# GpSimd for some sums and operand differences, 48 ones columns for the row sums, and three changes of order

## The chip, the core and the metric

The kernel runs on one core of a Trainium2 chip. The metric is the time of the whole kernel on the device in microseconds (us). Three runs of the kernel before took 2451.98, 2453.47 and 2453.75 us; their median, 2453.47, is the time before. A profiled execution gives a trace: start, length and the reason for waiting of each instruction on TensorE (PE, with its weight loads as PEld), VectorE (DVE), ScalarE (ACT), GpSimd (POOL) and SyncE (SP, which only issues transfers here).

## What is computed

One step of a hybrid decoder layer on 1024 prompt tokens and 64 sample tokens (T = 1088 rows of 1024 values), in float32:

```python
def ffn_half(x, nw, wg, wu, wd):
    h = rmsnorm(x, nw)
    return x + 0.5 * ((jax.nn.silu(h @ wg) * (h @ wu)) @ wd)
# x = ffn_half(x, first weights)
# u = rmsnorm(x) @ w_in;  x = x + concat(NSA(u_att), Mamba2(u_ssm)) @ w_out
# x = ffn_half(x, second weights);  y = rmsnorm(x)
```

`rmsnorm` divides each row by the root of its mean square (over 1024 values) and multiplies by a weight. NSA is an attention with three branches, Mamba2 a scan over chunks; neither is changed. The feed-forwards have an inner width of 2816 and are the bulk of the work.

## The kernel before, in words

**Products.** Every float32 operand is split into two parts that TensorE takes at full rate: `hi` (a rounded copy, by ScalarE or VectorE, line L267) and `lo` (the rest, a subtraction, L270). A product is then three matmuls, hi by hi, hi by lo and lo by hi (`mm3`, L250 to L252). The feed-forwards' products go by the Strassen-Winograd scheme: seven half-size products in place of eight, whose operands are sums and differences of the quarters of x and of the weights.

**Layout.** x lies with its features on the partitions (eight blocks of 128) and the tokens in the free dimension. The tokens come in two halves of 544; each half is worked on in two ranges, `z = 0` (256 tokens) and `z = 1` (288). A feed-forward's right operands are the tiles `B1` to `B7`, hi and lo (`B1h`, `B1l`), each for four pairs of row blocks `kk`. For one `kk`, `b_quad` splits the four quarters into B1 to B4, and `b_rest` makes four differences in place (rows `h<-h,h`, or `xT<-xT` and `T<-xT` before the second feed-forward) and splits three of them into B5, B6, B7. `First` is the first gate or up product of a feed-forward, which runs on B1 to B4 alone (eight plain products, L412 to L414), so it can start before the differences are there.

**Gate and up, then down.** `gate_up` runs 11 pairs of products p. Its outputs are tiles `Cc`; VectorE and ScalarE take them from PSUM (L375 to L386), ScalarE applies silu (L471), VectorE multiplies by half of the gate (L474). `g_factors` makes from each result the seven operands of the down projection, splits them, and stores hi and lo to a DRAM tensor `GD` (L442, L443). `Down` loads them back (`db`, L562) with the weights (`dw`, L552), makes weight sums `ds` and splits `da`, and runs the products `dq` (L633 to L635), which are added to x (`xT`, L642).

**w_out and the second norm.** x is updated by eight row blocks of w_out for the second token range at the end of the middle part (the loop over `j` below). For each row block there are 12 matmuls (`wout`), an evacuation (L2349), a square on ScalarE (L2351, into the tiles `hp` and `hpc`, which will hold the normalised rows later), and matmuls with a column of ones that add the squares up over the partitions (`nps`, L2353). `rms_row` makes from the sums the reciprocal roots and spreads them over the partitions with matmuls `nR` (L228); `h_half` (L2330) then makes the normalised rows. Weights for the last five row blocks are loaded (`out_raw`, L1907) and split (L2345) in the loop, three buffers deep. B1 to B7 of the first token range of the second feed-forward are made beside it, and its `First` gate `g` follows.

**Order.** The program is written in a framework that reorders the instructions of each engine by a simulated timeline of its own, under the dependences and under hints: `with tc.issue_after(x)` keeps what is inside behind instruction x. Engines run their instructions in order and wait for each other by semaphores; SP's queue is in order as well. So a change in one place moves instructions in others.

## Time and profile before

| | |
|---|---|
| runs (us) | 2451.98, 2453.47, 2453.75 |
| profiled execution (us) | 2458.56 |
| its span, first to last instruction (us) | 2456.9 |
| mean granted TensorE clock | 0.985 of full |
| GpSimd's busy time (us), instructions | 442.9, 556 |
| all transfers | 379.07 MB |

A row of the trace by time reads: start in us from the span's start, length in us, engine, line, operation, output tile <- inputs, partitions x elements, count of equal neighbours in one row; in brackets the idle time ahead of it and what ended it. A count's length goes from the first start to the last end. Equal instructions overlap a little, so two of 0.41 us take 0.74. A row of the table by stretches has the busy time and number of instructions of each engine, then the granted clock, the busy share of the DMA engines and GB/s.

### The profile page before, as it was taken

What the parts mean: (1) busy time and instruction counts of PE and PEld (TensorE: products, weight loads), DVE (VectorE), ACT (ScalarE), POOL (GpSimd) and SP (SyncE); (2) the same over time, 40 slices, a digit from 0 to 9 for tenths busy, and PEclk for the clock granted to TensorE, in tenths of its full rate; (3) what the DMA queues carried; (4) which work ended last, traced back from release to release, by engine and by line L of the source; (5) the groups of instructions that cost most, each with busy time, mean ns of one, the idle gap of its engine ahead of it and who ended that gap; (6) DMA issues with size and microseconds to landing.
All of it is one profiled execution on the core that took longest, in us unless ns stands there. A gap on an engine that the chain in (4) does not pass through costs nothing.

```text
span 2456.9 us, 48129 instructions
## 1 busy us (share of the span) xinstructions
PE 2394.8 (97%) x18866; PEld 2224.7 (91%) x18866; DVE 1748.7 (71%) x3833; ACT 1134.3 (46%) x2501; POOL 442.9 (18%) x556
## 2 busy tenths in 40 slices
PE   7999999999999999999999999999999999999998
PEld 6999999999999999998777775777999999999998
DVE  6767676768767855565767676778876777768776
ACT  7545444441124245333766767445544444443113
POOL 0000000011125343352545444011000000001110
PEclk9899999999999999999999999999899999999999
DMA  4434343488662333333212114476234443469654
GB/s 158 140 121 173 122 171 121 156 320 315 238 214 75 137 107 109 118 91 128 69 35 70 35 45 162 132 254 225 64 136 150 136 159 128 168 233 363 235 206 153
DMA packets 233903, 379.07 MB, mean 154 GB/s; under 512 B 18893, under 2 KB 148089, under 8 KB 233292
## 3 DMA queue, kind: packets, MB, share of 16 engines
q1 hardware_dynamic: 210248, 318.02, 38.0%
q0 software_dynamic: 11056, 38.59, 4.9%
q10 hardware_dynamic: 12372, 19.38, 2.2%
q8 instruction: 149, 2.44, 0.4%
q14 instruction: 78, 0.64, 0.1%
HBM read 255.66 MB, written 124.40 MB: 155 GB/s over the span
## 4 chain that ended last, share of the span: by engine, by line
PE 87%; DVE 5%; DMA 3%; ACT 3%; issue 1%; POOL 0%; SPq 0%; ACTq 0%; DVEq 0%; POOLq 0%
PE gY L367 6%; PE gY L366 6%; PE gY L368 6%; PE dq L633 6%; PE dq L634 6%; PE dq L635 6%; PE gX L367 5%; PE gX L366 5%; PE gX L368 5%; PE o L1862 3%; PE pT L1853 3%; PE g L414 1%; PE xbc L250 1%; PE g L412 1%; PE xbc L251 1%; PE xbc L252 1%
## 5 line engine op out<-in xcount | busy, mean ns | idle before, releaser
L633 PE MATMUL dq<-db,da 128*128 128x256 f32 (+1 forms) x1232 | 350.0, 288 | 5.0 <-DMA db<-GD 2.3
L634 PE MATMUL dq<-db,da 128*128 128x256 f32 (+1 forms) x1232 | 353.3, 288 | 0.0
L635 PE MATMUL dq<-db,da 128*128 128x256 f32 (+1 forms) x1232 | 353.0, 288 | 0.0
L270 POOL TENSOR_TENSOR ds<-dw 128x512 f32<-128x512 f32 x22 | 29.1, 1321 | 1231.8 <-DMA dw<-in_ffn_wd_dram 509.0
L642 DVE TENSOR_TENSOR xT<-xT,dq 128x256 f32<-128x256 f32 (+1 forms) x456 | 187.4, 433 | 87.1 <-PE dq L635 85.5
L633 PEld LDWEIGHTS dq<-db,da 128*128 128x128 f32 x1232 | 230.6, 189 | 6.1 <-ACT da L267 2.7
L635 PEld LDWEIGHTS dq<-db,da 128*128 128x128 f32 x1232 | 232.9, 189 | 0.0
L634 PEld LDWEIGHTS dq<-db,da 128*128 128x128 f32 x1232 | 231.9, 188 | 0.1
L267 ACT CAST whi<-ws 128x512 fp32r<-128x512 f32 x156 | 96.5, 623 | 206.0 <-PE gY L368 137.9
L270 DVE TENSOR_TENSOR wlo<-raw,whi 128x512 fp32r<-128x512 f32 x184 | 125.6, 687 | 82.8 <-ACT whi L267 82.5
L267 ACT CAST da<-ds 128x512 fp32r<-128x512 f32 x88 | 52.6, 623 | 236.0 <-PE dq L635 94.0
L267 ACT CAST whi<-raw 128x512 fp32r<-128x512 f32 x181 | 112.4, 625 | 71.9 <-PE wout L252 20.3
L270 DVE TENSOR_TENSOR wlo<-ws,whi 128x512 fp32r<-128x512 f32 x156 | 106.7, 687 | 42.4 <-ACT whi L267 39.8
L1826 DVE CUSTOM_DVE_ANT_0 pb<-s,mrow 128x384 f32<-128x384 f32 (+3 forms) x160 | 78.2, 513 | 32.5 <-PE pT L1853 15.7
L1853 PEld LDWEIGHTS pT<-ident,pb 128*128 128x128 f32 x528 | 60.3, 142 | 45.3 <-issue 37.3
L1831 ACT ACTIVATE pb<-pb,mx 128x384 f32<-128x384 f32 (+3 forms) x160 | 92.1, 577 | 17.4 <-DVE mx L1826 9.5
L366 PE MATMUL gY<-B3h,whi 128*128 128x256 f32 (+1 forms) x320 | 91.5, 286 | 1.4 <-ACT whi L267 1.4
L277 POOL TENSOR_TENSOR pb<-pb,sm 128x640 f32<-128x640 f32 (+7 forms) x70 | 84.6, 1232 | 44.2 <-DVE sm L1838 21.0
L366 PE MATMUL gX<-B6h,whi 128*128 128x256 f32 (+1 forms) x320 | 91.3, 286 | 0.7 <-ACT Cc L373 0.7
L367 PE MATMUL gX<-B6h,wlo 128*128 128x256 f32 (+1 forms) x320 | 91.4, 286 | 0.6 <-DVE wlo L270 0.6
L367 PE MATMUL gY<-B3h,wlo 128*128 128x256 f32 (+1 forms) x320 | 91.6, 287 | 0.2 <-DVE wlo L270 0.2
L367 PE MATMUL gY<-B2h,wlo 128*128 128x256 f32 (+1 forms) x320 | 91.4, 286 | 0.0
(762 smaller groups left out, 8542.1 us busy)
## 6 DMA issues: line engine op xcount, KB each, us to landing
db<-GD SPq DMA_DIRECT2D x42, 1632.0 KB
GD<-Cc SPq DMA_DIRECT2D x154, 272.0 KB
GD<-his SPq DMA_DIRECT2D x84, 272.0 KB
raw<-in_ffn_wu_dram SPq DMA_DIRECT2D x22, 1024.0 KB
dw<-in_ffn_wd_dram SPq DMA_DIRECT2D x44, 512.0 KB
raw<-in_ffn_wg_dram SPq DMA_DIRECT2D x21, 1024.0 KB
GD<-hp SPq DMA_DIRECT2D x70, 272.0 KB
db<-GD SPq DMA_DIRECT2D x14, 1088.0 KB
```

The costliest lines, as they stand in the source:

```text
L267: return nc.scalar.copy(out, src) if eng == "a" else ENGINES[eng].tensor_copy(out, src)
L270: ENGINES[eng].tensor_tensor(out, x, y, op=op)
L277: nc.gpsimd.tensor_tensor(out, x, by.to_broadcast(list(x.shape)), op=OP.mult)
L366: nc.tensor.matmul(q, ah[:, k], b_, start=first, stop=False, skip_group_check=True)
L367: nc.tensor.matmul(q, al[:, k], b_, start=False, stop=False, skip_group_check=True)
L368: nc.tensor.matmul(q, ah[:, k], c_, start=False, stop=(k == 3), skip_group_check=True)
L633: nc.tensor.matmul(q, x, bh[:, u, o], start=first, stop=False, skip_group_check=True)
L634: nc.tensor.matmul(q, y, bh[:, u, o], start=False, stop=False, skip_group_check=True)
L635: nc.tensor.matmul(q, x, bl[:, u, o], start=False, stop=(u == np_ - 1), skip_group_check=True)
L642: nc.vector.tensor_tensor(x, x, q, op=OP.subtract if i == 4 else OP.add)
L1831: nc.scalar.activation(p_, s if mask is None else p_, AF.Exp, bias=mx[:, 0:1], scale=1.0 if mask is None else -1.0, accum_out=part[:, hh_, ...
L1853: nc.tensor.transpose(tq_[:kn, P * hh_:P * hh_ + P], src, ident)
```

## The change

1. The row sums of squares (`rms_row`, `gate_sums`) are matmuls with 48 columns of ones (one column, broadcast) in place of one; the first column of each group is read.
2. In the last w_out loop the 24 matmuls `nps` (two records each in the trace) go. GpSimd adds the eight squares up in SBUF (seven additions of 128x288) and one `rms_row` on the total takes three matmuls at the end.
3. `rms_row` is cut in two, `rms_columns` (up to the reciprocal) and `rms_out` (the matmuls `nR`); for the first token range of the second norm `rms_out` is issued behind the seventh row block's products.
4. The loads of the second feed-forward's first gate and up weights (1 MB each) are issued on SP's queue behind the last two w_out loads (256 KB each), one behind each.
5. `b_rest` takes an engine: for every second row block GpSimd makes the four differences (eight of 128x256 and eight of 128x288 before the first feed-forward, eight of 128x256 before the second).
6. For the second-last p, `g_factors` makes all differences first and stores the operands in the order 6, 7, 5, 4, 1, 2, 3.

```diff
@@ -24,6 +24,7 @@
 KD = DM // P
 FB = 2816 // P
 HALF = T // 2
+NW = 48
 SUBS = [(0, 256), (256, 288)]
 CHUNKS = [(0, 384), (384, 384), (768, 320)]
 XCHUNKS = [(h * HALF + o, n) for o, n in SUBS for h in range(2)]
@@ -219,15 +220,17 @@
 
     roots = []
 
-    def norm_rows(r, parts, R):
+    def norm_columns(r):
 
         nc.vector.tensor_scalar(r, r, 1.0 / DM, EPS, op0=OP.mult, op1=OP.add)
         root = nc.scalar.activation(r, r, AF.Sqrt)
         nc.vector.reciprocal(r, r)
+        roots.append(root.ins)
+
+    def norm_rows(r, parts, R):
         for i, p0, c0, m in parts:
             nc.tensor.matmul(R[:, c0:c0 + m], r[p0:p0 + m, i:i + 1].to_broadcast([m, P]), ident[p0:p0 + m, p0:p0 + m],
                              start=True, stop=True, skip_group_check=True)
-        roots.append(root.ins)
         return R
 
     def wsplit(W, loads, early=False, dve=False):
@@ -249,7 +252,7 @@
     def mm3(q, w, xh, xl, first, last):
         nc.tensor.matmul(q, w[0], xh, start=first, stop=False)
         nc.tensor.matmul(q, w[1], xh, start=False, stop=False)
-        nc.tensor.matmul(q, w[0], xl, start=False, stop=last)
+        return nc.tensor.matmul(q, w[0], xl, start=False, stop=last)
 
     def dense(q, w, t0, n):
         for k in range(KD):
@@ -442,6 +445,15 @@
             nc.sync.dma_start(at[:, 0], f32(hi))
             nc.sync.dma_start(at[:, 1], src)
         sub("v", t1, b12, b11)
+        if p == FB // 2 - 2:
+            sub("v", t2, b22, t1)
+            yield
+            sub("v", t3, b22, b12)
+            sub("v", t4, t2, b21)
+            for x in ((6, t2), (7, t3), (5, t1), (4, t4), (1, b11), (2, b21), (3, b22)):
+                yield
+                put(*x)
+            return
         put(1, b11)
         yield
         sub("v", t2, b22, t1)
@@ -678,6 +690,7 @@
                                      accum_out=r2[p0:p0 + m, z, i:i + 1])
             parts.append((i, p0, c0, m))
         nc.vector.tensor_tensor(r, r2[:, 0], r2[:, 1], op=OP.add)
+        norm_columns(r)
         norm_rows(r, parts, R)
         Rs[t0] = FX.tile("xRs", [P, 288], 2)
         nc.scalar.copy(Rs[t0][:, :n], R[:, :n])
@@ -710,7 +723,7 @@
             due.append(x_block(s, kk))
             product(kk)
             if kk in (1, 2):
-                b_rest(s, *due.pop(0))
+                b_rest(s, *due.pop(0), "vp"[kk - 1])
         return due
 
     def late():
@@ -748,7 +761,7 @@
             u.run(0, kk, bankx, heng="v" if kk else "a")
             if kk < 2:
                 x_rms(HALF * kk + c0, n)
-                b_rest(0, *due.pop(0))
+                b_rest(0, *due.pop(0), "vp"[kk])
         with tc.issue_after(roots[-1]):
             g.finish(0)
         u.run(0, 3, bankx, heng="v")
@@ -758,7 +771,7 @@
         for kk in range(4):
             u.run(1, kk, banky)
             if kk in (0, 1):
-                b_rest(1, *due.pop(0))
+                b_rest(1, *due.pop(0), "vp"[kk])
         b_last(1)
         return [g, u]
 
@@ -840,26 +853,31 @@
         else:
             late_rows.append(m)
 
-    def rms_row(v, n, q=None, out=None):
-        out = v if out is None else out
-
+    def rms_row(v, n, out=None):
+        rms_out(*rms_columns(v, n), v if out is None else out)
+
+    def rms_columns(v, n):
         parts = blocks(n)
-        if q is None:
-            q = side("nps")
-            for i, m in parts:
-                nc.tensor.matmul(q[:m, i:i + 1], v[:, P * i:P * i + m], ones[:, :1], start=True, stop=True,
-                                 skip_group_check=True)
+        q = side("nps")
+        for i, m in parts:
+            nc.tensor.matmul(q[:m, NW * i:NW * i + NW], v[:, P * i:P * i + m], ones.to_broadcast([P, NW]), start=True,
+                             stop=True, skip_group_check=True)
+        sums = q[:, :NW * len(parts)].rearrange("p (i w) -> p i w", w=NW)[:, :, 0]
         r = NP.tile([P, len(parts)], F32, name="nr")
         if n % P:
             nc.vector.memset(r, 1.0)
-            nc.vector.tensor_copy(r[:n % P, n // P:], q[:n % P, n // P:len(parts)])
-        nc.vector.tensor_copy(r[:, :n // P], q[:, :n // P])
+            nc.vector.tensor_copy(r[:n % P, n // P:], sums[:n % P, n // P:])
+        nc.vector.tensor_copy(r[:, :n // P], sums[:, :n // P])
+        norm_columns(r)
+        return r, q, parts, n
+
+    def rms_out(r, q, parts, n, out):
         R = norm_rows(r, [(i, 0, P * i, m) for i, m in parts[:4]], side("nR"))
         nc.scalar.copy(out[:, :min(512, n)], R[:, :min(512, n)])
         for i, m in parts[4:]:
-            nc.tensor.matmul(q[:, 8:8 + m], r[:m, i:i + 1].to_broadcast([m, P]), ident[:m, :m],
+            nc.tensor.matmul(q[:, 256:256 + m], r[:m, i:i + 1].to_broadcast([m, P]), ident[:m, :m],
                              start=True, stop=True, skip_group_check=True)
-            nc.scalar.copy(out[:, 512:n], q[:, 8:8 + m])
+            nc.scalar.copy(out[:, 512:n], q[:, 256:256 + m])
 
     with pool("psum_dn", bufs=8, space=PSUM) as PD:
         adds = D1.add_x()
@@ -1347,12 +1365,13 @@
         for j, c in enumerate(cs):
             L = P if c < 8 else TS
             for g in range(2):
-                nc.tensor.matmul(q[:L, 2 * j + g:2 * j + g + 1], hs[:, j, g, :L], ones[:, :1], start=True, stop=True,
-                                 skip_group_check=True)
+                nc.tensor.matmul(q[:L, NW * (2 * j + g):NW * (2 * j + g) + NW], hs[:, j, g, :L], ones.to_broadcast([P, NW]),
+                                 start=True, stop=True, skip_group_check=True)
+        q = q[:, :6 * NW].rearrange("p (c g w) -> p c g w", g=2, w=NW)[:, :, :, 0]
         n = len(cs) - (8 in cs)
-        nc.vector.tensor_copy(yr[:, cs[0]:cs[0] + n], q[:, :2 * n].rearrange("p (c g) -> p c g", g=2))
+        nc.vector.tensor_copy(yr[:, cs[0]:cs[0] + n], q[:, :n])
         if 8 in cs:
-            nc.vector.tensor_copy(yr[:TS, 8], q[:TS, 2 * n:2 * n + 2])
+            nc.vector.tensor_copy(yr[:TS, 8], q[:TS, n])
 
     def gate_norm(yr):
         nc.vector.tensor_scalar(yr, yr, 1.0 / 256, EPS, op0=OP.mult, op1=OP.add)
@@ -1902,10 +1921,12 @@
     def two(v):
         return v.rearrange("p (b t) -> p b t", b=2)
 
+    out_loads = []
+
     def out_raw(k0, m):
         raw = WA.tile([P, 4, P], F32, name="raw", bufs=3)
-        nc.sync.dma_start(raw, A["w_out"][0][512 * k0:512 * k0 + 512, P * m:P * m + P].rearrange(
-            "(k p) f -> p k f", p=P))
+        out_loads.append(nc.sync.dma_start(raw, A["w_out"][0][512 * k0:512 * k0 + 512, P * m:P * m + P].rearrange(
+            "(k p) f -> p k f", p=P)))
         return raw
 
     def out_w(W, k0, m, eng="v", raw=None):
@@ -2234,8 +2255,8 @@
     def side(name):
         return PO.tile([P, 512], F32, name=name, tag="wout")
 
-    def x2_rms(z, q=None):
-        rms_row(acc2[z], 2 * SUBS[z][1], q)
+    def x2_rms(z):
+        rms_row(acc2[z], 2 * SUBS[z][1])
         c0, n = SUBS[z]
         for b in range(2):
             for m in range(0, KD, 4):
@@ -2330,15 +2351,17 @@
         nc.vector.scalar_tensor_tensor(rows[m][:, r], X2[1][:, m, r], wn2[:, m:m + 1], acc[:, r],
                                        op0=OP.mult, op1=OP.mult)
 
-    rms_row(a0, 288, out=acc)
+    first = rms_columns(a0, 288)
     h0 = [h_of(X2[0][:, kk], X2[0][:, kk + 4]) for kk in range(4)]
-    sums = side("nps")
     ws = kept[5:]
     raws = [out_raw(0, m) for m in MB[:3]]
     for j, m in enumerate(MB[5:] + MB[:5]):
         q = (PO if j < 6 else PL).tile([P, 512], F32, name="wout")[:, :288]
         for k in range(4):
-            mm3(q, (ws[j][0][:, k], ws[j][1][:, k]), ha[0][:, k], ha[1][:, k], k == 0, k == 3)
+            done = mm3(q, (ws[j][0][:, k], ws[j][1][:, k]), ha[0][:, k], ha[1][:, k], k == 0, k == 3)
+        if j == 6:
+            with tc.issue_after(done.ins):
+                rms_out(*first, acc)
         if j < 5:
             raw = raws[j] if j < 3 else out_raw(0, MB[j])
             hi, lo = (WA.tile([P, 4, P], F32R, name=nm_) for nm_ in ("whi", "wlo"))
@@ -2349,9 +2372,10 @@
         nc.vector.tensor_tensor(X2[1][:, m, b1_], X2[1][:, m, b1_], q, op=OP.add)
         sq = rows[m][:, b1_]
         nc.scalar.activation(sq, X2[1][:, m, b1_], AF.Square)
-        for i, n in blocks(288):
-            nc.tensor.matmul(sums[:n, i:i + 1], sq[:, P * i:P * i + n], ones[:, :1], start=(j == 0 and i == 0),
-                             stop=(j == KD - 1), skip_group_check=True)
+        if j:
+            nc.gpsimd.tensor_tensor(total, total, sq, op=OP.add)
+        else:
+            total = sq
     for i, a in ((4, 2), (3, 3), (1, 0), (2, 1)):
         for kk in range(4):
             hi, lo = (t[:, kk] for t in BN[0][i])
@@ -2365,12 +2389,12 @@
                     copy("a", hi, src)
                 with tc.issue_after(behind[1].ins):
                     sub("v", lo, src, f32(hi))
-    rms_row(acc[:, b1_], 288, sums)
+    rms_row(total, 288, out=acc[:, b1_])
     for m in range(0, KD, 4):
         nc.sync.dma_start(xD[:, m:m + 4, HALF + 256:T], X2[1][:, m:m + 4, b1_])
     with tc.issue_after(behind[1].ins):
         for kk in range(4):
-            b_rest(0, kk, h0[kk])
+            b_rest(0, kk, h0[kk], "vp"[kk % 2])
     for kk in range(4):
         for m in (kk, kk + 4):
             with tc.issue_after(behind[1].ins):
@@ -2392,7 +2416,8 @@
         return PY.tile([P, 512], F32, name=name, tag="Y", bufs=4)
 
     def begin2():
-        g = First(F1, A["ffn2_wg"][0], silu_out)
+        with tc.issue_after(out_loads[-2].ins):
+            g = First(F1, A["ffn2_wg"][0], silu_out)
         for kk in range(4):
             g.run(0, kk, bankx)
         h1 = [h_of(rows[kk], rows[kk + 4]) for kk in range(4)]
@@ -2400,7 +2425,8 @@
             b_quad(1, kk, h1[kk])
         for kk in range(2):
             b_rest(1, kk, h1[kk])
-        u = First(F1, A["ffn2_wu"][0], times_out(g))
+        with tc.issue_after(out_loads[-1].ins):
+            u = First(F1, A["ffn2_wu"][0], times_out(g))
         for kk in range(4):
             u.run(0, kk, bankx)
         for kk in range(2, 4):
```

How this moves instructions, at three places (lines of the changed program are some 3 to 23 higher: L270 is L273 there, L250 to L252 are L253 to L255, L228 is L232, L2349 is L2372, L386 is L389, L384 is L387, L474 is L486).

TensorE at the end of w_out, before: the sums stand between the sixth row block's last matmul and the seventh's first.

```order
L252 MATMUL wout<-ol,whi 128x288
L228 MATMUL nR<-ident,nr 128x128 x2
L228 MATMUL nR<-ident,nr 128x32
L2353 MATMUL nps<-ones,hp 128x1 x2
L2353 MATMUL nps<-ones,hp 32x1
L2353 MATMUL nps<-ones,hp 128x1 x2
L2353 MATMUL nps<-ones,hp 32x1
L2353 MATMUL nps<-ones,hpc 128x1 x2
L2353 MATMUL nps<-ones,hpc 32x1
```

TensorE there after, from the seventh row block's last matmuls on.

```order
L255 MATMUL wout<-ol,whi 128x288
L232 MATMUL nR<-ident,nr 128x128 x2
L232 MATMUL nR<-ident,nr 128x32
L254 MATMUL wout<-oh,wlo 128x288
L255 MATMUL wout<-ol,whi 128x288
```

The matmuls `nR` have moved behind the seventh block, and no sums are left there; three `nps` of 48 columns come 28 matmuls of the gate later.

GpSimd between the sample attention's gathers and the down projection's `ds`, after (before, nothing stands there). `hp<-hp` rows are the additions of squares, the others differences.

```order
L2376 TENSOR_TENSOR hp<-hp 128x288
L273 TENSOR_TENSOR xT_19998<-xT_19998 128x256 x3
L2376 TENSOR_TENSOR hp<-hp,hpc 128x288
L273 TENSOR_TENSOR xT_19998<-xT_19998 128x256 x2
L2376 TENSOR_TENSOR hp<-hp 128x288
L273 TENSOR_TENSOR T_21000<-xT_19998 128x256
L273 TENSOR_TENSOR xT_19998<-xT_19998 128x256
L2376 TENSOR_TENSOR hp<-hp 128x288
L273 TENSOR_TENSOR T_21000<-xT_19998 128x256
L2376 TENSOR_TENSOR hp<-hp 128x288
L2376 TENSOR_TENSOR hp<-hp,hpc 128x288 x2
```

Fifteen instructions are new on GpSimd there, in the order in which they run; the eight differences were on VectorE's queue, between the splits of the second feed-forward's operands.

VectorE at the first feed-forward's end, where the down projection's weights are prepared between the last evacuations, before:

```order
L270 TENSOR_TENSOR da_6240<-dw_6248,da_6240 128x512
L384 TENSOR_TENSOR Cc<-Cc,gY 128x288
L386 TENSOR_TENSOR Cc<-Cc,gY 128x288
L270 TENSOR_TENSOR ds_6272<-dw_6248,dw_6252 128x512
L474 SCALAR_TENSOR_TENSOR Cc<-Cc 128x1088
L386 TENSOR_TENSOR Cc<-Cc,gY 128x256
L270 TENSOR_TENSOR ds_6276<-ds_6272,dw_6248 128x512
L270 TENSOR_TENSOR Cc<-Cc 128x544
L386 TENSOR_TENSOR Cc<-Cc,gY 128x288
```

and after:

```order
L486 SCALAR_TENSOR_TENSOR Cc<-Cc 128x1088
L389 TENSOR_TENSOR Cc<-Cc,gY 128x256
L273 TENSOR_TENSOR Cc<-Cc 128x544
L273 TENSOR_TENSOR da_6240<-dw_6248,da_6240 128x512
L389 TENSOR_TENSOR Cc<-Cc,gY 128x288
L273 TENSOR_TENSOR Cc<-Cc,his 128x544
L273 TENSOR_TENSOR ds_6272<-dw_6248,dw_6252 128x512
L389 TENSOR_TENSOR Cc<-Cc,gY 128x256
L273 TENSOR_TENSOR ds_6276<-ds_6272,dw_6248 128x512
L389 TENSOR_TENSOR Cc<-Cc,gY 128x288
```

The multiplication over 1088 tokens, the difference and one evacuation that stood behind the split of the weights `dw_6248` now stand ahead of it.

## The prediction

> **What bounds the kernel now.** I read the page's busy shares and chain first, then the table by stretches at the places that the change touches, then single instructions there.
>
> ```profile
> span 2456.9 us, 48129 instructions
> PE 2394.8 (97%) x18866; PEld 2224.7 (91%) x18866; DVE 1748.7 (71%) x3833; ACT 1134.3 (46%) x2501; POOL 442.9 (18%) x556
> PE 87%; DVE 5%; DMA 3%; ACT 3%; issue 1%; POOL 0%; SPq 0%; ACTq 0%; DVEq 0%; POOLq 0%
> 20.00:40.00 20.00, 17.50 (x129) 16.31 (x128) 19.44 (x55) 15.31 (x47) 0.00 (x0) 0.91 0.50 156
> 515.00:520.00 5.00, 2.86 (x12) 2.86 (x13) 4.96 (x9) 2.65 (x6) 0.00 (x0) 0.72 1.03 356
> 1719.00:1743.00 24.00, 20.46 (x107) 19.78 (x107) 21.20 (x59) 12.14 (x35) 0.00 (x0) 0.64 0.31 104
> ```
>
> TensorE is busy 97% of 2456.9 us and stands for 87% of the chain, so only stretches where it waits, or runs at a low granted clock, can be shortened. The stretch rows (PE, PEld, DVE, ACT, POOL busy, clock, DMA share, GB/s) show three that the change touches: the first feed-forward's beginning (VectorE 19.44 of 20 us), its hand-over to the down projection (clock 0.72), and the end of w_out (clock 0.64). GpSimd does nothing in any of them. The profiled execution took 2458.56 us; the runs' median is 2453.47, so I subtract from 2453.5. The measurement tells 0.2%, or 4.9 us, from no change.
>
> **The end of w_out, where most of the change lies.**
>
> ```profile
> 1720.65 1.04 PE L228 MATMUL nR<-ident,nr 128*128 128x128 f32 x6 [1.59 <-DVE nr L226]
> 1721.63 1.98 PE L2353 MATMUL nps<-ones,hp 128*128 128x1 f32 x12
> 1724.67 3.47 PE L2353 MATMUL nps<-ones,hp 128*128 128x1 f32 x18
> 1728.07 0.85 PE L250 MATMUL wout<-oh,whi 128*128 128x288 f32 x2
> 1735.60 2.27 PE L2353 MATMUL nps<-ones,hpc 128*128 128x1 f32 x12 [1.96 <-ACT hpc L2351]
> 1737.79 0.58 PE L413 MATMUL g<-B1h,wlo 128*128 128x256 f32 x1
> 1742.44 0.33 PE L414 MATMUL g<-B3l,whi 128*128 128x256 f32 x1
> 1742.60 0.28 PE L412 MATMUL g<-B1h,whi 128*128 128x256 f32 x1
> ```
>
> The removed sums occupy TensorE from 1721.63 to 1728.07 and from 1735.60 to 1737.79: 6.4 + 2.2 us, at half clock. It looks like 8.6 us to gain. But the real work behind them waits for VectorE, whose queue has no gap here:
>
> ```profile
> 1717.03 0.74 DVE L270 TENSOR_TENSOR B2l<-xT,B2h 128x256 fp32r<-128x256 f32 x2
> 1719.41 0.74 DVE L270 TENSOR_TENSOR xT<-xT 128x256 f32<-128x256 f32 x2
> 1720.08 0.43 DVE L2349 TENSOR_TENSOR xT<-xT,wout 128x288 f32<-128x288 f32 x1
> 1725.50 0.67 DVE L2345 TENSOR_TENSOR wlo<-raw,whi 128x512 fp32r<-128x512 f32 x1
> 1734.29 2.48 DVE L270 TENSOR_TENSOR wlo<-raw,whi 128x512 fp32r<-128x512 f32 x4
> ```
>
> The first of the four splits at 1734.29, with the usual 0.69 us, ends at 1734.98; the second feed-forward's gate cannot multiply with it sooner, though the 12 sums ahead of it held it until 1737.79. So what counts is when this split ends. Two subtractions of 128x256 take 0.74 us and one 0.41, so one costs 0.335 in the queue. The change takes eight of them (blocks 1 and 3) out from ahead of the split: 8 x 0.335 = 2.7 us, and 1734.98 becomes 1732.3. The h rows and evacuations stay ahead of it, and the earlier w_out load helps the next-to-last product only if VectorE lets it.
>
> Against that stand fourteen GpSimd instructions, eight subtractions and six of the seven sums, in the same stretch; the last sum follows the last product. Their price is read elsewhere:
>
> ```profile
> 737.02 0.77 DVE L823 SCALAR_TENSOR_TENSOR hl<-xT,vec,hh 128x544 fp32r<-128x544 f32 x1
> 730.51 0.41 DVE L642 TENSOR_TENSOR xT<-xT,dq 128x256 f32<-128x256 f32 x1
> 730.90 1.42 DVE L823 SCALAR_TENSOR_TENSOR hl<-xT,vec,hh 128x544 fp32r<-128x544 f32 x1
> 729.95 1.79 POOL L270 TENSOR_TENSOR ds<-dw,ds 128x512 f32<-128x512 f32 x1
> 731.71 1.85 POOL L816 TENSOR_TENSOR rms<-rms,scr 128x544 f32<-128x544 f32 x1
> 985.62 0.74 POOL L270 TENSOR_TENSOR ea<-ea,xbc 128x256 f32<-128x256 f32 x1
> ```
>
> A VectorE operation with both inputs in SBUF takes 0.77 us alone, and 1.42 beside GpSimd: it starts at 730.90 and ends at 732.32, 0.58 after the GpSimd one (729.95 + 1.79) is done. The next GpSimd one, issued at 731.71, takes 1.85 and waits in turn for that VectorE operation. The evacuation at 730.51, with an input in PSUM, keeps its 0.41 inside GpSimd's 1.79. So the two take turns, one instruction each, and a GpSimd instruction holds VectorE for its length less the start-up that both hide in waiting, about 0.14 (0.74 becomes 0.60). The SBUF — State Buffer page of the Trainium skill, section "SBUF: two separate sides", says the same of two SBUF inputs against a GpSimd operation that reads SBUF: whichever starts first holds the shared ports for the whole instruction and the other blocks. By that rule the sum is the one that I make here, and by a split of bandwidth it would be the first rival; the rows bear the rule out.
>
> Fourteen times 0.60 is 8.4 us. About 2 us of it falls beside evacuations and waits (six evacuations like the one at 1720.08, 0.37 each in the queue), which leaves 6.4: the split ends not at 1732.3 but at 1738.7. The next-to-last product's own split is late in the same way. From the 1717.03 row the new order has one subtraction and one evacuation more (0.7), then 0.67 + 0.37 + 1.0 + 0.1 + 0.34 + 0.6 up to its end: 1720.8. Ten of the fourteen stand ahead of it, 6.0 less 0.8 of cover: 1726. So TensorE stands idle about 7 us from 1719 and comes out at half clock. The gate's first 22 matmuls then run from about 1739.0 at 0.214 us to the next edge of the clock at 1742.5 (16 of them), six more at 0.114: done at 1743.2, against 1742.55 now. Net **+0.7 us**. Ends: without any turn-taking 1732.3, 16 matmuls at half clock to the edge at 1735.7 and six at full, 1736.4: -6. With a full 0.74 and no cover, 14 x 0.74 = 10.4: the split ends at 1742.7, 22 x 0.214 more, 1747.4: +5. I stay by the middle, since the rows show both the turns and the cover.
>
> What follows there is hidden: the new sum needs the last square, GpSimd's addition (0.74 x 288/256 = 0.83) and six short matmuls; 28 gate matmuls (28 x 0.114 = 3.2 us or more) stand ahead of it on TensorE, and its norm is needed only by the second token range. If that cover went it would cost up to 2 us. On SP's queue the first w_out load now goes ahead of the two 1 MB loads, so gate's raw comes some 2 us later; it is cast at 1726.88 now and would have 10 us to spare.
>
> **48 columns.** No row has 48, but both neighbours:
>
> ```profile
> L850 PE MATMUL nps<-ones,acc x14: 165/250/250, 1623.4 to 1713.3; 128*128 128x1 f32 x12, 128*32 128x1 f32 x2
> L228 PE MATMUL nR<-ident,nr x36: 270/275/376, 763.6 to 1745.5; 128*128 128x128 f32 x32, 32*128 32x32 f32 x4
> ```
>
> One column takes 250 ns, 128 take 275, so a widened one costs 0 to 0.025 us; some 70 remain, 0 to 1.8 us. I take 0: the weight load sets the pace. The splitting of the norm reorders, and moves a few matmuls past nine others: 0 +-1.
>
> **The hand-over to the down projection.**
>
> ```profile
> 511.31 1.31 DVE L270 TENSOR_TENSOR da<-dw,da 128x512 fp32r<-128x512 f32 x1 [1.67 <-ACT da L267]
> 512.54 0.44 DVE L384 TENSOR_TENSOR Cc<-Cc,gY 128x288 f32<-128x288 f32 x1
> 513.27 0.68 DVE L270 TENSOR_TENSOR ds<-dw,dw 128x512 f32<-128x512 f32 x1
> 513.87 1.28 DVE L474 SCALAR_TENSOR_TENSOR Cc<-Cc 128x1088 f32<-128x1088 f32 x1
> 515.07 0.41 DVE L386 TENSOR_TENSOR Cc<-Cc,gY 128x256 f32<-128x256 f32 x1
> 516.64 0.44 DVE L386 TENSOR_TENSOR Cc<-Cc,gY 128x288 f32<-128x288 f32 x1
> 517.01 0.72 DVE L270 TENSOR_TENSOR Cc<-Cc,his 128x544 fp32r<-128x544 f32 x1
> 517.14 0.58 PE L633 MATMUL dq<-db,da 128*128 128x256 f32 x1 [2.26 <-DVE Cc L386]
> 513.73:517.15 3.42, 1.16 (x11) 0.93 (x9) 3.42 (x7) 2.44 (x5) 0.00 (x0) 1.00 0.74 272
> 517.15:520.56 3.41, 3.41 (x15) 3.41 (x16) 3.37 (x5) 1.54 (x4) 0.00 (x0) 0.50 1.01 312
> 540.00:545.00 5.00, 5.00 (x42) 5.00 (x41) 3.65 (x9) 1.24 (x2) 1.29 (x1) 1.00 0.74 241
> 555.00:560.00 5.00, 4.28 (x35) 4.05 (x33) 5.00 (x12) 0.62 (x2) 0.00 (x0) 1.00 1.02 402
> ```
>
> A wait for a transfer stops VectorE until 511.31, and what is queued behind it makes the last evacuation late (516.64), for which TensorE stands 2.26 us and loses the clock for the next 3.41 us (0.50, 1.7 us of work). In the new order the halving (L474, 1.28) stands ahead of the waiting instruction, and five things between 512.54 and the last evacuation: two evacuations (0.44, 0.41), a Cc remainder (0.72) and two ds (0.68), each about 0.08 less in the queue, 2.53 together. So it starts at 515.07, 1.57 earlier. TensorE's wait falls to 0.69, the stretch is busy for four fifths, and the half clock goes: -1.57 - 1.7 = -3.3. But the DMA engines are at 1.01 to 1.03 in the rows from 515 and from 555, with 0.74 between at 540 to 545, and the next wait is already theirs: within 555 to 560 TensorE is busy 4.28 of 5. A TensorE that is 3.3 us early meets transfers that are at most 1.5 early. I take **-1.5**, ends 0 and -3.3. The second feed-forward's hand-over gets the same order, at full clock: 0 to -1, **-0.3**.
>
> **The two beginnings.** Of sixteen subtractions in the first, four or five fall where VectorE is the bound (up to 37 us): each saves 0.335 there and holds VectorE 0.60 when it meets an operation with two SBUF inputs, about six in ten: 5 x (0.36 - 0.335) is nothing, ends -1.5 and +1.3. The others lie beside TensorE that is busy throughout (50 to 77 us) and are hidden; if that cover goes, eleven times 0.27 are 3 us. I take **+0.3**.
>
> The sum: 0.7 - 1.5 - 0.3 + 0.3 = -0.8, **2452.7 us**, within 0.2%.
>
> **Rivals.** First, GpSimd costs VectorE next to nothing: -6 at w_out, and with the hand-overs' -1.8 to -3.6 some 2445. The evacuation row at 730.51 speaks for it, the slow rows against it. Second, the turns cost their full length: +5 at w_out, +2 in the beginnings, -1.8 at the hand-overs: 2458.7. It decides once the blocked time exceeds some 8 us of the stretch; the chained dependences (ScalarE casts what GpSimd subtracts, in a fixed order) speak for it, the evacuations against. Third, w_out as I have it, but the transfers follow, and the hand-overs bring 3.3 + 1: 2450.2, still within the bound. Fourth, a half-clock stretch comes or goes elsewhere (each 1.7 us); it widens all cases. A page rule bears on it: TensorE: Matmul & The Clock Gate in the Trainium skill, Part 1, gives an idle window of about 3.4 us as the cause of half rate; the 3.41 us above agree.
>
> **How the numbers follow.** My case with the third: 0.53, of which the fourth carries 0.04 beyond the bound on either side. First rival 0.27, of it 0.24 beyond; second 0.20, of it 0.16 beyond. That makes faster 0.28, same 0.52 (0.45 + 0.03 + 0.04), slower 0.20. Eight in ten lie from 2445 to 2459, the ends of the first two rivals; the likeliest case alone goes from 2449 to 2456.
>
> **What would show it.** Right: VectorE's operations with two SBUF inputs at 1719 to 1738 take 0.6 to 1.0 instead of 0.41; TensorE idles 6 us or more there; the gate starts within 1.5 us of 1739 on today's scale; the half clock at 517 is gone; the wait for db near 559 has grown. Wrong: VectorE's durations there stay 0.41, or the gate starts before 1736.

## The result, and the profile after

The changed kernel takes 2465.27 us (median of 7 runs, 2459.56 to 2475.15), the kernel before 2452.96 in runs beside it (7 runs, 2447.99 to 2454.37): a ratio of 1.0051, interval 1.0036 to 1.0066. It is slower by half a per cent, outside the predicted range. The profiled execution took 2470.7 us, its span is 2469.0.

The page's first lines and the same three stretches as before:

```profile
span 2469.0 us, 48067 instructions
PE 2384.9 (97%) x18824; PEld 2215.2 (90%) x18824; DVE 1753.4 (71%) x3809; ACT 1133.2 (46%) x2501; POOL 471.4 (19%) x587
PE 83%; DMA 6%; DVE 6%; ACT 3%; issue 1%; POOL 0%; SPq 0%; ACTq 0%; DVEq 0%; POOLq 0%
20.00:40.00 20.00, 17.04 (x119) 15.94 (x119) 18.31 (x47) 14.77 (x46) 4.83 (x6) 0.83 0.46 146
515.00:520.00 5.00, 5.00 (x43) 5.00 (x41) 3.32 (x6) 3.21 (x9) 1.29 (x1) 1.00 0.99 339
1719.00:1743.00 24.00, 16.15 (x94) 14.40 (x92) 24.00 (x53) 15.95 (x40) 12.11 (x13) 0.85 0.49 159
```

TensorE is busy 9.9 us less than before in a span that is 12.1 longer, and DMA's share of the chain has doubled, from 3 to 6%. At 515 TensorE no longer stands and has its full clock (as it has in a second profile of the kernel before, told of below). At w_out's end VectorE has no gap in 24 us, beside 12.11 us of GpSimd.

To see where time goes, equal matmuls of TensorE are paired between two profiles, and the difference of their starts is followed: a **shift**, the median over slices of 25 us. Against the profile shown of before, the shift is -2.5 us behind the first beginning, -6.5 at 600, -6.95 at 1575, **+8.5 at 1700**, +11.55 at 1800 and +12.1 at the end. So most of the loss is made between 1580 and 1700, in the sample attention, a stretch that the prediction does not speak of. These are two rows of it, of the changed kernel, and then of a second profile of the kernel before (span 2455.4 us, the twelfth run below):

```profile
1620.00:1640.00 20.00, 16.04 (x164) 14.12 (x165) 13.68 (x35) 6.46 (x13) 5.12 (x5) 0.91 0.65 211
1680.00:1700.00 20.00, 14.78 (x128) 11.24 (x127) 10.42 (x36) 7.03 (x17) 2.67 (x3) 0.87 0.77 238
```

```profile
1620.00:1640.00 20.00, 20.00 (x256) 16.45 (x256) 18.07 (x47) 9.40 (x17) 7.93 (x7) 1.00 0.84 267
1680.00:1700.00 20.00, 17.79 (x184) 11.19 (x182) 11.77 (x36) 8.18 (x20) 1.38 (x2) 1.00 0.52 165
```

Nothing of the change is written there. But the framework's simulated timeline orders this stretch differently: by a count in the two traces (rows with the same operation, tiles and shape, in order), some 105 of VectorE's 558 rows between 1450 and 1716 stand elsewhere. In the list of the waits of TensorE and VectorE between 1580 and 1715 (us in total, times, longest) the changed kernel has

```profile
PE kT_ps L2092 <- DMA schk<-in_cache_win_dram: 3.9, 1, 3.9
PE sPT_ps L2150 <- DVE pcT L270: 3.1, 1, 3.1
PE so L2160 <- DVE sPT L270: 2.0, 3, 1.0
PE so L2157 <- DVE sPT L270: 1.9, 1, 1.9
DVE xs L2301 <- DMA xs<-xD: 6.7, 3, 3.7
```

and these are the places of the two long ones, by time, VectorE's ahead of TensorE's:

```profile
1697.71 0.46 DVE L2301 TENSOR_TENSOR xs<-xs,wout 128x288 f32<-128x288 f32 x1 [3.72 <-DMA xs<-xD]
1698.08 0.28 DVE L270 COPY pcT<-sPT_ps 127x128 f32<-127x128 f32 x1
1698.51 1.09 PE L2150 MATMUL sPT_ps<-ident,S 128*128 128x128 f32 x4 [3.10 <-DVE pcT L270]
1623.48 1.11 PE L2092 MATMUL kT_ps<-ident,schk 128*128 128x128 f32 x4 [3.94 <-DMA schk<-in_cache_win_dram]
```

The rows `xs` of x go from DRAM through w_out's addition back to DRAM, three buffers deep. At 1697.71 VectorE stands 3.72 us for such a load; the copy `pcT`, on which TensorE waits, is queued behind it. In the second profile of before the corresponding wait totals 2.1 us, and TensorE never waits longer than 0.5 us for VectorE there:

```profile
PE kT_ps L2071 <- DMA schk<-in_cache_sel_dram,idx: 2.7, 4, 1.8
PE so L2139 <- DVE sPT L267: 0.5, 1, 0.5
DVE xs L2280 <- DMA xs<-xD: 2.1, 1, 2.1
```

The four waits shown of the changed kernel's TensorE make 10.9 us, to which come three stretches of 3.41 us at half clock (from 1623.28, 1694.96 and 1698.37). Set against the second profile of before, waits and half clock are nearly the whole loss: between the places of 1575 and 1700 TensorE stands 12.4 us instead of 3.5, and of its 10.2 us at half clock, where that profile has none, it is busy 6.9, which is 3.5 us of work. The 8.9 and the 3.5 make 12.4 of the 13.0 us that the table below gives.

### The profile page after: what moved, and what is told of

It is laid out like the page before. It is cut to its first block, busy times and chain, and to the rows that moved or that the text cites. A ratio compares the mean times of both kernels' runs of the same rounds, so it can differ in the third digit from the quotient of the medians.

```text
span 2469.0 us, 48067 instructions
## 1 busy us (share of the span) xinstructions
PE 2384.9 (97%) x18824; PEld 2215.2 (90%) x18824; DVE 1753.4 (71%) x3809; ACT 1133.2 (46%) x2501; POOL 471.4 (19%) x587
## 4 chain that ended last, share of the span: by engine, by line
PE 83%; DMA 6%; DVE 6%; ACT 3%; issue 1%; POOL 0%; SPq 0%; ACTq 0%; DVEq 0%; POOLq 0%
PE gY L370 6%; PE gY L371 6%; PE gY L369 6%; PE dq L645 6%; PE dq L646 6%; PE dq L647 6%; PE gX L370 5%; PE gX L369 5%; PE gX L371 5%; PE o L1881 3%; PE pT L1872 3%; PE xbc L253 1%; PE xbc L254 1%; PE xbc L255 1%; DMA schk<-in_cache_sel_dram,idx 1%
## 5 line engine op out<-in xcount | busy, mean ns | idle before, releaser
L273 POOL TENSOR_TENSOR ds<-dw 128x512 f32<-128x512 f32 x22 | 29.4, 1337 | 1096.5 <-DMA dw<-in_ffn_wd_dram 880.4
L270 ACT CAST whi<-ws 128x512 fp32r<-128x512 f32 x156 | 96.4, 623 | 208.1 <-PE gY L371 137.5
L273 DVE TENSOR_TENSOR wlo<-raw,whi 128x512 fp32r<-128x512 f32 x184 | 126.4, 693 | 83.6 <-ACT whi L270 83.5
L270 ACT CAST da<-ds 128x512 fp32r<-128x512 f32 x88 | 52.3, 624 | 235.8 <-issue 96.0
L270 ACT CAST whi<-raw 128x512 fp32r<-128x512 f32 x181 | 112.3, 625 | 78.3 <-PE wout L255 22.0
L273 DVE TENSOR_TENSOR wlo<-ws,whi 128x512 fp32r<-128x512 f32 x156 | 106.7, 688 | 44.4 <-ACT whi L270 44.0
L369 PE MATMUL gY<-B2h,whi 128*128 128x256 f32 (+1 forms) x320 | 91.4, 286 | 0.0
```

Of the source, the lines that this page charges most:

```text
L270: return nc.scalar.copy(out, src) if eng == "a" else ENGINES[eng].tensor_copy(out, src)
L273: ENGINES[eng].tensor_tensor(out, x, y, op=op)
L369: nc.tensor.matmul(q, ah[:, k], b_, start=first, stop=False, skip_group_check=True)
```

## The experiments

One table for all runs. The columns are what each stretch added to the shift, in us, against the **second** profile of before, since the first has half clock from 52.94 to 76.83 which no other run with an unchanged beginning shows for so long. That second execution took 2457.09 us, some 3.5 above the median of the runs beside it, so a total that is worked out from the table looks that much better than the times do. The last two are the median time and its ratio to before with the interval.

| run | to 75 | 75 to 600 | 600 to 1575 | 1575 to 1700 | 1700 to 1800 | rest | us | ratio |
|---|---|---|---|---|---|---|---|---|
| the change | 1.4 | -2.9 | -1.5 | **13.0** | 2.5 | 1.1 | 2465.27 | 1.0051 (1.0036 to 1.0066) |
| e1 beginning + hand-over | 2.5 | -3.9 | -0.8 | **15.1** | -3.1 | 0.1 | 2464.68 | 1.0046 (1.0033 to 1.0060) |
| e2 w_out parts | 0.6 | 0.4 | -0.3 | -1.3 | **6.5** | 4.0 | 2464.78 | 1.0052 (1.0038 to 1.0066) |
| e3 hand-over | -0.2 | -3.2 | 3.3 | -2.4 | -1.6 | 0.2 | 2453.30 | 1.0001 (0.9991 to 1.0012) |
| e4 beginning | 1.9 | -1.2 | 1.8 | -0.9 | -0.1 | 0.9 | 2459.86 | 1.0035 (1.0022 to 1.0048) |
| e5 sums on VectorE | 1.5 | 0.4 | -3.0 | -0.9 | -0.4 | -0.3 | 2456.69 | 1.0011 (1.0000 to 1.0023) |
| e6 sums on TensorE | -0.2 | -0.5 | -2.6 | 0.6 | -1.4 | 1.2 | 2454.07 | 1.0004 (0.9989 to 1.0019) |
| e7 GpSimd sums only | 1.0 | -0.6 | 1.7 | -1.3 | 1.9 | 2.6 | 2457.89 | 1.0025 (1.0011 to 1.0040) |
| e8 all but 48 and hand-over | 2.0 | 0.4 | 2.7 | -1.7 | 4.4 | 0.4 | 2465.08 | 1.0047 (1.0031 to 1.0062) |
| e9 change, sums on VectorE | 0.9 | -3.6 | -1.3 | **12.6** | 0.2 | 0.4 | 2467.47 | 1.0062 (1.0045 to 1.0079) |
| e10 no GpSimd sums, no beginning | -0.5 | -2.7 | -1.9 | -0.7 | -1.2 | 0.1 | 2448.97 | 0.9985 (0.9976 to 0.9994) |
| e11 48 + hand-over | 1.1 | -3.4 | -2.0 | -0.6 | -1.0 | -0.4 | 2450.73 | 0.9998 (0.9987 to 1.0010) |
| e13 change, four xs | 2.1 | -3.8 | -3.7 | 7.9 | 4.8 | 0.3 | 2467.18 | 1.0051 (1.0032 to 1.0069) |
| e14 e10, four xs | -0.2 | -3.6 | -2.7 | 1.7 | -1.4 | 0.3 | 2450.61 | 0.9986 (0.9974 to 0.9998) |

The middle column (600 to 1575) holds code that none of the runs means to touch, and it goes from -3.7 to +3.3, with stretches of half clock that come and go. That is what one profile can be off by, so only larger differences, or ones that several runs repeat, are read as causes below.

**Is it the order in the sample attention?** First two halves of the change: the first beginning and the hand-overs (the first half of part 5, and 6), and w_out with the second beginning (2, 3, 4 and the second half of 5), each with one column of ones.

```diff
 e1: before, with
+                b_rest(s, *due.pop(0), "vp"[kk - 1])
+                b_rest(0, *due.pop(0), "vp"[kk])
+                b_rest(1, *due.pop(0), "vp"[kk])
+        if p == FB // 2 - 2:
```

> Only two parts of the change: GpSimd's differences in the first feed-forward's beginning, and the other order of the second-last p's operands. Nothing at the end of w_out, one ones column. But the scheduler now puts the sample attention (some 1600 to 1700 us) in nearly the order of the changed kernel. Theory A (the lost time comes from the order of matmuls in the sample attention): the two parts win 2.5 + 4 us by 750 us and lose 12 to 16 between 1580 and 1710: 2453 - 6.5 + 14 = about 2460. Theory B (it comes from GpSimd's work and the new sum at the end of w_out): 2453 - 6.5 = about 2446.5, no loss between 1580 and 1710.

```diff
 e2: the change, with
-NW = 48
+NW = 1
-                b_rest(s, *due.pop(0), "vp"[kk - 1])
+                b_rest(s, *due.pop(0))
-                b_rest(0, *due.pop(0), "vp"[kk])
+                b_rest(0, *due.pop(0))
-                b_rest(1, *due.pop(0), "vp"[kk])
+                b_rest(1, *due.pop(0))
-        if p == FB // 2 - 2:
+        if p < 0:
```

> Only the parts at the end of w_out: squares summed by GpSimd, the first norm's matmuls moved, w_out loads ahead of the 1 MB loads, GpSimd's eight differences before the second feed-forward. One ones column. The sample attention keeps the order of the kernel before. Theory A: no loss between 1580 and 1700, and 0.7 to 5 us (3 in the changed kernel's trace) at the end of w_out: 2454 to 2458. Theory B: 12 to 18 us slower, 2465 to 2471.

e1 has the new order in the sample attention and lost 15.1 us there, without any edit between 600 and 1700 (its time, 2464.68, is above the 2460 of its theory A, whose beginning was to win 2.5 us and lost as much). e2 has the old order, lost nothing there, but 6.5 us at the end of w_out. So there are two losses, not one. (e2's time, 2464.78, is that of its theory B, whose place is wrong. Another 4.0 us of its profile are lost behind 1800, all of it between 2150 and 2225, at the second feed-forward's hand-over, with half clock from 2189.8 to 2196.6; e7 below loses 2.2 in the same place. Why is not shown.) Then the two halves of e1, each alone; both have the old order in the sample attention.

```diff
 e3: before, with
+        if p == FB // 2 - 2:
 e4: before, with
+                b_rest(s, *due.pop(0), "vp"[kk - 1])
+                b_rest(0, *due.pop(0), "vp"[kk])
+                b_rest(1, *due.pop(0), "vp"[kk])
```

> Only the other order of the second-last p's operands. The sample attention keeps its order but for a few VectorE rows. From the changed kernel's trace the hand-over at 500 to 530 us wins 3.3 to 4 us, and the half-clock stretch at 517 us is gone: theory A says 2449 to 2450. If the hand-over's gain belonged to GpSimd's differences in the beginning instead (theory B of this step), 2453.

> Only GpSimd's sixteen differences in the first feed-forward's beginning. The sample attention keeps its order. From the changed kernel's trace: 2.5 us faster by 80 us and no change after that, 2450.5. The prediction's step said +0.3 (2453.5).

Neither loses anything between 1575 and 1700, though together they lose 15.1 there. e3 gains its 3 us at the hand-over and has given them back by 975, with half clock from 762 and from 981, where the second profile of before has none; its time is the same as before, not the 2449 to 2450 of its theory A. e4 came out 9 us above what was expected of it. Its beginning costs 1.9 us, against 0.4 in the mean of the eight runs with an unchanged beginning; the six runs with GpSimd there have 0.9 to 2.5, 1.8 in the mean, so the part costs some 1.4 us. In all its profile lies 2.5 us behind the second one of before, which with that one's 3.5 makes the 6 of its time; only the 1.4 to 1.9 are found at the beginning, the rest stays open.

Last the counter-test: nearly everything in, but a combination for which the order in the sample attention stays the old one.

```diff
 e8: the change, with
-NW = 48
+NW = 1
-        if p == FB // 2 - 2:
+        if p < 0:
```

> All of the change but the 48 columns and the new order at the hand-overs. In this one the lists of instructions in the sample attention (1580 to 1710) stand as in the kernel before, although GpSimd's differences in the first beginning are in. Theory 'the 15 to 17 us at 1580 to 1710 come from the order in those lists': they are gone, within 2 us of before there; w_out's end loses 5 to 8 us, the beginning 1 to 2: 2463 to 2467 in all. Rival 'the GpSimd work of the beginnings, or a run's chance, makes that loss, whatever the order': some 15 us lost between 1580 and 1710 again, 2475 or more.

It lost nothing between 1575 and 1700 (-1.7) with all GpSimd work in. In all sixteen profiles the stretch costs 7.9 to 15.1 us in the four with the new order (the change, e1, e9, e13) and -2.5 to 1.7 in the twelve others. By the count used above, 104 to 111 of VectorE's 558 rows moved in those four, and 0 to 9 in eleven of the others; the twelfth, e14, has a third order (97 moved) and is told of next.

**What in the new order costs it?** One more xs buffer, in the changed kernel (e13) and in e10, told of below (e14). The first pair of lines stands for three places in the program.

```diff
-        xs = WA.tile([P, 576], F32, name="xs", bufs=3)
+        xs = WA.tile([P, 576], F32, name="xs", bufs=4)
-            pg = KC.tile([P, 128], F32, name="pg")
+            pg = KC.tile([P, 128], F32, name="pg", bufs=1)
```

> The whole change with four buffers for the rows that w_out's second part loads, adds to and stores again (xs: load from DRAM, addition, store), instead of three; one small tile of the sample attention (pg) has one buffer instead of two to make room. The lists keep the changed kernel's order up to the place from which the rows are loaded ahead. Theory 'in the new order TensorE and VectorE stand behind round trips of xs through DRAM (VectorE waits 6.7 us for such loads there, in a second profile of the kernel before 2.1)': the loads start a buffer earlier, those waits go, and of 13 to 15 us between 1580 and 1710 some 5 to 8 come back; 2456 to 2461 in all. Rival 'the order of the sample attention's own chain (keys, scores, probabilities) makes the loss, xs only stands in it': under 2 us come back, 2463 to 2467.

> The kernel of the tenth run (48 columns, later norm, order of loads, second beginning's differences on GpSimd, new order at the hand-overs; no sums on GpSimd, first beginning on VectorE) with four xs buffers in the same way. That kernel waits little for xs, as the kernel before does (2.1 us of VectorE, little of it on the path): 2447 to 2449, no difference. Rival: the fourth buffer moves the order of the sample attention again, and 5 us or more are lost there.

In e13 VectorE waits for xs loads as little as in the kernel before, and the waits on `pcT` are gone:

```profile
DVE xs L2301 <- DMA xs<-xD: 2.3, 1, 2.3
PE kT_ps L2092 <- DMA schk<-in_cache_sel_dram,idx: 6.1, 5, 2.6
PE kT_ps L2092 <- DMA schk<-in_cache_win_dram: 2.5, 1, 2.5
```

The stretch costs 7.9 us instead of 13.0. That the 5 us were the round trips is likely but not shown: the fourth buffer changed the lists as well (33 of VectorE's 516 rows between 1450 and 1716 stand elsewhere than in the changed kernel). The rest is in waits for the gathered keys (`schk`, 8.6 us in all), which the new order makes longer and which this run does not explain. The time did not follow: 2467.18 us, since 2.3 us more were lost at w_out's end in its profile, and the rest is not visible in it. So these waits are seen to go in their place, and their worth in the total is not shown. In e14 the fourth buffer moved 104 of VectorE's 544 rows between 1450 and 1716 against e10, about as many as the change moves, and the time is no different from e10's (2450.61; the stretch costs 1.7 us against -0.7). So it is not reordering as such that costs 13 us, but this order; which of its moves do it stays open.

**The end of w_out.** e2 says that the w_out parts cost 6.5 us by themselves. Three runs take them apart. In e5 VectorE makes the seven sums of squares, in e6 TensorE as before, and only the eight differences are GpSimd's; in e7 only the sums are.

```diff
 e5: e2, with
-            nc.gpsimd.tensor_tensor(total, total, sq, op=OP.add)
+            nc.vector.tensor_tensor(total, total, sq, op=OP.add)
 e6: e2, with the accumulating matmuls nps of the kernel before
 e7: e2, with
-            b_rest(0, kk, h0[kk], "vp"[kk % 2])
+            b_rest(0, kk, h0[kk])
```

> The earlier run of the w_out parts (sums and differences on GpSimd, one ones column, before's order in the sample attention) lost 7.0 us between 1710 and 1775 and ended at 2464.8. Here the seven sums of squares are VectorE's, at 0.41 us each (0.335 in its queue: 2.3 us), and only the eight differences of the second feed-forward's first operands stay with GpSimd. Theory 'turns, and a dense VectorE stream keeps GpSimd out': the sum that stood 6.06 us on GpSimd while VectorE ran without a gap takes 0.41 us, six blockings of some 0.6 us are gone; the stretch 1710 to 1775 loses 2 to 4 us instead of 7, in all some 2460. Rival 'the place of the instructions does not matter, the order of the split and the casts does': 7 us lost again, some 2464 to 2466.

> As the run before, but the sums of squares stay with TensorE in the accumulating form of the kernel before; the norm's later place, the order of the loads and the eight differences on GpSimd are kept. Theory 'turns': eight blockings of 0.6 us against eight subtractions of 0.335 saved, +2.1 us, and TensorE has its sums again, which lie in time in which it waits anyway: the stretch 1710 to 1775 loses 1 to 3 us, in all 2455 to 2458. Rival 'GpSimd's differences are the whole loss, the sums nothing': 6 to 7 us lost, 2460 to 2464.

> The sums on GpSimd, but all sixteen differences of the second feed-forward's first operands on VectorE as before. Theory 'turns': six blockings of 0.6 us with nothing saved on VectorE's list, 3 to 4 us; the last sum waits on GpSimd for a gap in VectorE's stream again (3 to 6 us, of which what the gate's matmuls do not cover shows): 4 to 7 us lost from 1710 to 1800, 2459 to 2463. Rival 'the differences are the whole loss': 0 to 1, 2453 to 2455.

From 6.5 us the loss goes to -0.4 (sums on VectorE) and -1.4 (on TensorE): without GpSimd's sums it is gone. The differences alone on GpSimd cost nothing here, and the sums alone 1.9, so the 6.5 belong to the two together. All three runs lost less in this place than was expected of them (2 to 4, 1 to 3 and 4 to 7 us). That the two do not add up has a likely reason in GpSimd's rows, first e2's, then e5's:

```profile
1714.55 1.86 POOL L273 TENSOR_TENSOR xT<-xT 128x256 f32<-128x256 f32 x1 [32.41 <-DVE B1l L273]
1726.49 0.97 POOL L2376 TENSOR_TENSOR hp<-hp 128x288 f32<-128x288 f32 x1
1736.36 6.06 POOL L2376 TENSOR_TENSOR hp<-hp,hpc 128x288 f32<-128x288 f32 x1 [4.88 <-ACT hpc L2374]
```

```profile
1712.99 6.25 POOL L273 TENSOR_TENSOR xT<-xT 128x256 f32<-128x256 f32 x6 [33.19 <-DVE B1l L273]
1719.20 2.05 POOL L273 TENSOR_TENSOR T<-xT 128x256 f32<-128x256 f32 x2
```

In e5 GpSimd is done after 8.3 us, and VectorE has the rest of the loop to itself. In e2 GpSimd's thirteen instructions run without a gap from 1714.55 to 1727.46, and VectorE's splits, on which both the products and the gate wait, are slowed down all along. The last sum, at 1736.36, is the other way round: one addition takes 6.06 us, until VectorE's unbroken stream ends at 1741.76.

```profile
1735.99 2.49 DVE L273 TENSOR_TENSOR wlo<-raw,whi 128x512 fp32r<-128x512 f32 x4
1740.58 1.18 DVE L273 TENSOR_TENSOR B2l<-hp,B2h 128x288 fp32r<-128x288 f32 x3
1742.47 1.21 PE L863 MATMUL nps<-ones,hp 128*128 128x1 f32 x6 [1.32 <-POOL hp L2376]
```

Finally, the same exchange in the whole change, which keeps the new order in the sample attention:

```diff
 e9: the change, with
-            nc.gpsimd.tensor_tensor(total, total, sq, op=OP.add)
+            nc.vector.tensor_tensor(total, total, sq, op=OP.add)
```

> The whole change, but the sums of squares at the end of w_out are VectorE's instead of GpSimd's. The sample attention keeps the changed kernel's order. Theory 'two separate losses, the order in the sample attention (15.5 us) and GpSimd's sums at w_out (7 us alone, 3 in the changed kernel)': 14 to 17 us lost again between 1580 and 1710, at the end of w_out 0 to 1 instead of 3; 2461 to 2464. Rival 'the sums and the sample attention are one loss, through the filler matmuls of w_out that run out early': the sample attention recovers too, 2450 or less.

It loses 12.6 us in the sample attention again, and 0.2 at the end of w_out instead of 2.5: two separate losses. Its median of 2467.47 (2462.23 to 2474.65) lies above the expected 2461 to 2464, though: the 2.3 us that w_out's end has gained in the profile do not show in the time.

**The 48 columns, and a better version.**

```diff
 e10: the change, without the sums on GpSimd and without "vp" in the first beginning
 e11: before, with
+NW = 48
+        if p == FB // 2 - 2:
```

> What the runs so far found to be good or free: the 48 columns, the norm's later place, the loads' order, the differences of the second beginning on GpSimd, the new order at the hand-overs; the sums of squares stay with TensorE and the first beginning with VectorE. The lists in the sample attention stand as in the kernel before. If the pieces add up: the hand-over -4, the end of w_out -1, the sample attention 0, 48 columns 0 to 1.8: 2448 to 2451. If what is gained at the hand-over is given back to half-clock windows later, as it was with the new order at the hand-over alone: 2452 to 2454.

> The 48 columns and the new order at the hand-overs; nothing on GpSimd. The hand-over's order alone ended at 2453.3, no different from before. If a widened column costs nothing: 2453 again. If its 25 ns (275 for 250 in the changed kernel's rows) sets TensorE's pace: some 100 of them, 2.5 us more, 2456.

> The kernel before once more, for a second profile of it: the first one has half clock from 52.94 to 76.83, which the runs with an unchanged beginning (the hand-over alone, w_out alone) do not have. If that stretch was that execution's chance, this one is 3 to 4 us earlier by 80 us, and the comparisons of the beginning are to be made against it.

e11 (0.9998) is no different from e3 (1.0001): the widened columns cost nothing that can be told, though the intervals, about 0.0011 to each side, would hide the 2.5 us of the rival too. e10 is faster than the kernel before, 0.9985 (0.9976 to 0.9994), some 4 us, and faster than the change; it has what was good or free of it and the old order in the sample attention, and e14, nearly the same program, repeats it (0.9986). Which of its parts bring the 4 us isn't shown: e3, e6 and e11, with some of them each, are no different from before. e12, the kernel before again, lies 3.9 us ahead of the first profile by 75 us, as expected: the half clock there was that execution's.

## Why the prediction was wrong, by its steps

**"The splitting of the norm reorders, and moves a few matmuls past nine others: 0 +-1."** This is the step that failed. Only the places that the change touches were looked at; the reordering in the sample attention, which stands in the lists and could be seen there, got no term. It measured +15.5 us against the first profile (+13.0 against the second), more than the whole miss of 2465.27 - 2452.7 = 12.6. It isn't the splitting of the norm that does it either: e1 has none of that. What the runs showed in place of the 0 is the sample attention in a new order, in which TensorE stands 8.9 us more, mostly for transfers of keys and for results of VectorE, and runs 10.2 us at half clock.

**w_out's end, +0.7.** The steps to the gate were right. VectorE's rows with two SBUF inputs became long, as said:

```profile
1725.51 1.70 DVE L273 TENSOR_TENSOR B1l<-xT,B1h 128x256 fp32r<-128x256 f32 x2
1727.46 1.88 DVE L273 TENSOR_TENSOR B2l<-xT,B2h 128x256 fp32r<-128x256 f32 x2
1747.12 0.58 PE L416 MATMUL g<-B1h,wlo 128*128 128x256 f32 x1 [5.56 <-DVE wlo L273]
```

Two of them take 1.70 and 1.88 us for 0.74, TensorE stands 5.56 us for the gate's first split alone (6 or more were forecast for the whole stretch, where its waits come to 12.0; 3.5 before), and the gate starts at 1747.12, which less the shift of 8.53 is 1738.6 on the scale of before; 1739 was forecast. In e2 it is 1736.73 + 1.96 = 1738.7. What was mis-sized is what follows: the clock was to come back at the next edge, at 1742.5. In e2 the stretches from edge to edge (TensorE's busy time first, the clock behind the five engines) read

```profile
1732.42:1735.83 3.41, 0.00 (x0) 0.00 (x0) 3.41 (x10) 1.19 (x4) 0.00 (x0) 0.50 0.00 0
1735.83:1739.24 3.41, 2.51 (x12) 2.51 (x12) 3.41 (x8) 0.72 (x2) 2.88 (x1) 0.50 0.48 173
1739.24:1742.65 3.41, 2.09 (x10) 1.79 (x10) 2.52 (x7) 1.09 (x4) 3.18 (x1) 0.50 0.00 0
1742.65:1746.06 3.41, 3.41 (x17) 3.38 (x18) 1.25 (x5) 0.82 (x2) 0.00 (x0) 0.50 0.00 0
1746.06:1749.47 3.41, 3.41 (x18) 3.38 (x16) 0.00 (x0) 0.00 (x0) 0.00 (x0) 0.50 0.00 0
1749.47:1752.90 3.43, 3.43 (x29) 3.26 (x28) 2.36 (x6) 1.87 (x5) 0.00 (x0) 1.00 0.00 0
```

so the half clock lasts until 1749.47 + 1.96 = 1751.4, 8.9 us past the forecast edge. Less the wait of 1.32 in it and the six matmuls of the last sum that now stand in the gate (1.14 up to the next one's start), that is 6.5 us at half clock, 3.2 us of work; with the wait (1.3), the six matmuls (1.1) and the 0.7 of the forecast it makes 6.3 of the 7.0 by which e2 falls back there against the first profile (from -1.96 to +5.02); 0.7 stay open. In the changed kernel the clock comes back at 1752.98 - 8.53 = 1744.45, and the stretch costs 3.0.

**"What follows there is hidden."** In e2 it wasn't: the last sum takes 6.06 us, where 0.83 was counted, and TensorE waits 1.32 for it. In the changed kernel it was, all but the six matmuls themselves (0.75 us in the gate's stream): there the last but one is long, and the last takes 1.06.

```profile
1743.05 3.46 POOL L2376 TENSOR_TENSOR hp<-hp,hpc 128x288 f32<-128x288 f32 x1 [6.58 <-ACT hpc L2374]
1747.87 1.06 POOL L2376 TENSOR_TENSOR hp<-hp,hpc 128x288 f32<-128x288 f32 x1 [1.35 <-ACT hpc L2374]
1752.83 0.82 PE L863 MATMUL nps<-ones,hp 128*128 128x48 f32 x6
```

The prediction had GpSimd and VectorE take turns "one instruction each". The rows of 6.06 and 3.46 show that this can fail beside an unbroken VectorE stream; the 1.06, beside four splits without a gap, shows that it need not.

**The hand-over, -3.3 cut to -1.5.** In its place the uncut value came nearer: the eight runs with the new order add -2.7 to -3.9 between 75 and 600, the six without it +0.4 to -1.2. Of its two terms one is shown. TensorE's wait for the last evacuation fell from 2.26 us to 0.56 (0.69 was forecast). The other, the 1.7 us of half clock from 517, is not the old order's: of the eight profiles with that order three have it, and the second profile of before is not among them. It has no slack of the DMA engines at 540 either, and its TensorE has no wait for db near 559:

```profile
513.73:517.15 3.42, 3.42 (x30) 3.42 (x29) 3.38 (x5) 2.38 (x6) 0.00 (x0) 1.00 0.98 335
540.00:545.00 5.00, 5.00 (x42) 5.00 (x42) 3.92 (x9) 1.14 (x2) 1.29 (x1) 1.00 1.02 415
```

That the gain is some 3 us against this profile too, without the clock's term, is in part luck: TensorE's waits between 470 and 590 fall from 4.1 to 2.2 us, and about 1 us stays open. The reason given for the cut, that the wait for db would grow because the transfers cannot follow, failed as well; in the changed kernel

```profile
540.00:545.00 5.00, 5.00 (x43) 5.00 (x42) 4.38 (x11) 1.14 (x2) 1.09 (x1) 1.00 1.02 408
555.00:560.00 5.00, 5.00 (x43) 5.00 (x42) 4.21 (x9) 0.69 (x2) 0.00 (x0) 1.00 1.02 410
PE dq L645 <- DMA db<-GD: 0.3, 1, 0.3
```

the only wait for db there is one of 0.3 us, at 547.7, and near 559 there is none, where the first profile has 1.0. In the whole time the gain does not show: e3 and e11 have it in their profiles and are no different from before.

**The beginnings, +0.3** (-1.5 to +1.3, and 3 if the cover goes): some +1.4, just beyond the upper end. **48 columns, 0**: not contradicted; a widened matmul's median is 275 ns against 250, the upper end of what was forecast for one, and the total of 0 to 1.8 us is less than the runs can tell.

**The rivals.** The second (turns at full length, slower) came nearest in time, 2458.7, and its +5 at w_out lies between the change's 3.0 and e2's 7.0; but it isn't what decided. Without the sample attention's 13 us the profiled execution would have been level with the second one of before. The fourth, half clock elsewhere, carries part of that loss, as three such stretches of the sample attention (3.5 us of work).

## What to carry to other kernels

Where a scheduler orders the program by a simulated timeline, compare the whole lists of before and after first, and give each stretch whose order moved a term with a range of its own; here that term was larger than all others. Work moved to GpSimd beside a full VectorE must be costed twice, as time that VectorE loses and as time that GpSimd's own result comes late, and it pays only where nobody waits for either. Parts of a change that are free or good by themselves can lose together, so build the version without the bad parts: here e10 and e14 are the fastest.
